# RoPE over 16 heads on one core: fp16 products summed by TensorE against fp32 throughout, in place, by VectorE, GpSimd and TensorE

## The chip, the cores and the metric

The kernel runs on one core of one Trainium2 chip. The metric is the device time of one execution in microseconds (us). The profile's span, from the first to the last instruction, is some 1.5 to 2 us shorter.

## The reference

```python
# x: (16, 512, 1024) float32, 16 heads of 64; cos, sin: (512, 32)
x = x.reshape(batch, seq, num_heads, head_dim)
x1, x2 = x[..., :half_dim], x[..., half_dim:]
cos, sin = cos[None, :, None, :], sin[None, :, None, :]
out = concatenate([x1 * cos - x2 * sin, x1 * sin + x2 * cos], axis=-1)
```

Every output is a sum of two products: a = x · cos, and b = (x with its halves exchanged) · (−sin, +sin). So 33.55 MB are read, 33.55 MB written, and each element costs two multiplications and an addition.

## The kernel before

The load, issued from GpSimd, converts fp32 to fp16 on its way. VectorE makes both products in fp16, a batch (128 partitions x 4096) at a time. TensorE adds them: two matmuls by the identity accumulate in PSUM, the memory that TensorE writes. (The tiles lie in SBUF, the core's other on-chip memory.) ScalarE copies the fp32 sum out.

```python
xin = ctx.enter_context(tc.tile_pool(name="xin", bufs=3))
tmp = ctx.enter_context(tc.tile_pool(name="tmp", bufs=2))
orez = ctx.enter_context(tc.tile_pool(name="orez", bufs=3))
# ... tables in fp16, identity in fp16 ...
for bo in range(batch // BP):                       # BP = 2 batches per load
    x_sb = xin.tile([P, BP, KK, dim], FP16)
    nc.gpsimd.dma_start(out=x_sb, in_=x_v2[bo])
    for bi in range(BP):
        # ...
        nc.vector.tensor_tensor(out=A, in0=xb, in1=cosb, op=ALU.mult)
        nc.vector.tensor_tensor(out=Bt, in0=swap_view(xb), in1=snsb, op=ALU.mult)
        for c in range(FREE // CH):                 # CH = 512
            nc.tensor.matmul(out=ps, lhsT=ident, rhs=Aflat[:, sl], start=True, stop=False)
            nc.tensor.matmul(out=ps, lhsT=ident, rhs=Bflat[:, sl], start=False, stop=True)
            nc.scalar.copy(out=oflat[:, sl], in_=ps)
        nc.sync.dma_start(out=out_v[b], in_=o_sb)
```

Of the kernel before, what the change touches and what calls it, by code (L numbers as in the profile page):

```python
# [1 line left out]

# [5 lines left out]

FP32 = mybir.dt.float32  # L10
FP16 = mybir.dt.float16
ALU = mybir.AluOpType


@with_exitstack
def kernel(
    ctx: ExitStack,
    tc: tile.TileContext,
    x: bass.AP,
    cos: bass.AP,  # L20
    sin: bass.AP,
    num_heads: bass.AP,
    out: bass.AP,
):
    nc = tc.nc
    P = nc.NUM_PARTITIONS
    batch, seq, dim = x.shape
    nh = num_heads
    head_dim = dim // nh
    half = head_dim // 2  # L30

    KK = seq // P
    assert P * KK == seq
    FREE = KK * dim
    CH = 512
    assert FREE % CH == 0
    BP = 2
    assert batch % BP == 0

    x_v2 = x.rearrange("(bo bi) (p kk) d -> bo p bi kk d", bi=BP, kk=KK)  # L40
    out_v = out.rearrange("b (p kk) h d -> b p kk (h d)", kk=KK)
    cos_v = cos.rearrange("(p kk) j -> p kk j", kk=KK)
    sin_v = sin.rearrange("(p kk) j -> p kk j", kk=KK)

    fixed = ctx.enter_context(tc.tile_pool(name="fixed", bufs=1))
    xin = ctx.enter_context(tc.tile_pool(name="xin", bufs=3))
    tmp = ctx.enter_context(tc.tile_pool(name="tmp", bufs=2))
    orez = ctx.enter_context(tc.tile_pool(name="orez", bufs=3))
    psum = ctx.enter_context(tc.tile_pool(name="psum", bufs=4, space=bass.MemoryType.PSUM))

    ident = fixed.tile([P, P], FP16)
    make_identity(nc, ident)

    cos_sb = fixed.tile([P, KK, half], FP32)
    sin_sb = fixed.tile([P, KK, half], FP32)
    nc.sync.dma_start(out=cos_sb, in_=cos_v)
    nc.sync.dma_start(out=sin_sb, in_=sin_v)
    cos16 = fixed.tile([P, KK, half], FP16)
    sns16 = fixed.tile([P, KK, 2, half], FP16)
    nc.vector.tensor_copy(out=cos16, in_=cos_sb)  # L60
    nc.vector.tensor_scalar_mul(out=sns16[:, :, 0, :], in0=sin_sb, scalar1=-1.0)  # L61
    nc.vector.tensor_copy(out=sns16[:, :, 1, :], in_=sin_sb)  # L62

    cosb = bass.AP(
        tensor=cos16.tensor,
        offset=cos16.offset,
        ap=[cos16.ap[0], [half, KK], [0, nh * 2], [1, half]],
    )
    snsb = bass.AP(
        tensor=sns16.tensor,  # L70
        offset=sns16.offset,
        ap=[sns16.ap[0], [2 * half, KK], [0, nh], [1, 2 * half]],
    )

    def swap_view(x_sb):
        return bass.AP(
            tensor=x_sb.tensor,
            offset=x_sb.offset + half,
            ap=[x_sb.ap[0], [head_dim, KK * nh], [-half, 2], [1, half]],
        )  # L80

    for bo in range(batch // BP):
        x_sb = xin.tile([P, BP, KK, dim], FP16)
        nc.gpsimd.dma_start(out=x_sb, in_=x_v2[bo])  # L84
        for bi in range(BP):
            b = bo * BP + bi
            xb = x_sb[:, bi]

            A = tmp.tile([P, KK, dim], FP16, name="A")
            nc.vector.tensor_tensor(out=A, in0=xb, in1=cosb, op=ALU.mult)  # L90
            Bt = tmp.tile([P, KK, dim], FP16, name="Bt")
            nc.vector.tensor_tensor(out=Bt, in0=swap_view(xb), in1=snsb, op=ALU.mult)  # L92

            o_sb = orez.tile([P, KK, dim], FP32)
            Aflat = A.rearrange("p kk d -> p (kk d)")
            Bflat = Bt.rearrange("p kk d -> p (kk d)")
            oflat = o_sb.rearrange("p kk d -> p (kk d)")
            for c in range(FREE // CH):
                sl = slice(c * CH, (c + 1) * CH)
                ps = psum.tile([P, CH], FP32)  # L100
                nc.tensor.matmul(out=ps, lhsT=ident, rhs=Aflat[:, sl], start=True, stop=False)  # L101
                nc.tensor.matmul(out=ps, lhsT=ident, rhs=Bflat[:, sl], start=False, stop=True)  # L102
                nc.scalar.copy(out=oflat[:, sl], in_=ps)  # L103

            nc.sync.dma_start(out=out_v[b], in_=o_sb)


# [1 line left out]
_INS = ['x', 'cos', 'sin', 'num_heads']  # L109
_OUTS = [((16, 512, 16, 64), 'float32')]  # L110
#: Inputs that are plain numbers.
_NUMBERS = {'num_heads': 16}


# [26 lines left out]
```

## Time and profile before

| | before |
|---|---|
| median time | 165.67 us (2 runs, 165.66 to 165.68) |
| span of the profiled run | 164.1 us |
| busiest engine | TensorE, 54% |
| transfers (both queues) | 98.5% of the 16 engines' span |

The page of the profile. The first lines give the span and each engine's busy time. The DMA row is the busy share of the transfer engines in 40 equal slices of the span, in tenths; the queue lines give packets, MB and share; the line that starts with "DMA 71%" is the chain of waits that ended last.

```profile
span 164.1 us, 814 instructions
PE 88.6 (54%) x256; PEld 31.5 (19%) x256; DVE 72.5 (44%) x35; ACT 68.7 (42%) x129; POOL 6.5 (4%) x14
...
DMA  5999999999999999999999999999999999999992
...
q0 software_dynamic: 2176, 16.78, 49.7%
q1 hardware_dynamic: 2592, 33.69, 48.8%
...
HBM read 33.69 MB, written 33.55 MB: 410 GB/s over the span
...
DMA 71%; PE 11%; ACT 6%; DVE 3%; issue 1%; ACTq 0%; POOL 0%; POOLq 0%; DVEq 0%
```

The DMA row is full from the second slice to the last but one, and the two queues together are at 98.5%. The 67.2 MB move at 410 GB/s (the load queue's 16.78 MB are counted after the conversion to fp16). No engine is over 54% busy. What bounds this kernel is the transfers, and nearly nothing else.

In the profile PE is TensorE, DVE VectorE, ACT ScalarE, POOL GpSimd, and L103 is a line of the kernel. Two groups of instructions matter for costing the change, from the same page (count, busy us and mean ns of one, then the idle time before it).

```profile
L103 ACT COPY o_sb<-ps 128x512 f32<-128x512 f32 x128 | 67.4, 609 | 82.9 <-DMA out_dram<-o_sb 58.5
L90 DVE TENSOR_TENSOR A<-x_sb,cos 128x4096 f16<-128x4096 f16 x16 | 36.7, 2291 | 69.9 <-DMA x_sb<-in_x_dram 41.3
```

ScalarE copies 512 columns in 609 ns, from which its copies of 1024 were estimated. VectorE takes 2.29 us for 4096 fp16 elements. The timeline of TensorE (start, duration, instruction, idle time before) shows how the clock falls during idle time:

```profile
72.49 0.58 PE L101 MATMUL ps<-A,ident 128*128 128x512 f16 x1 [4.21 <-ACT o_sb L103]
72.87 0.63 PE L102 MATMUL ps<-Bt,ident 128*128 128x512 f16 x1
73.30 0.63 PE L101 MATMUL ps<-A,ident 128*128 128x512 f16 x1
...
77.50 0.38 PE L101 MATMUL ps<-A,ident 128*128 128x512 f16 x1
77.72 0.38 PE L102 MATMUL ps<-Bt,ident 128*128 128x512 f16 x1
```

After 4.2 us of idleness a 512-column fp16 matmul starts every 0.43 us. Five microseconds later it starts every 0.22 us.

### The profile page before, as it was taken

How to read it: one execution, taken by the hardware profiler on the slowest of the kernel's cores; microseconds unless marked ns; L12 is line 12 of the kernel's file. 1: busy time of each engine (PE TensorE's matmuls, PEld its weight loads, DVE VectorE, ACT ScalarE, POOL GpSimd, SP SyncE). 2: the span in 40 equal slices, each digit the busy share in tenths (PEclk: the TensorE clock that was granted, in tenths of full speed). 3: DMA queues.
4: the chain of work that ended last, by engine and by line, in shares of the span. 5: the costliest groups of instructions: out<-in, count | busy, mean ns of one | idle time of the engine just before them, and what ended most of it. 6: DMA issues, size and time to landing. Idle time of an engine off the chain costs nothing.

```text
span 164.1 us, 814 instructions
## 1 busy us (share of the span) xinstructions
PE 88.6 (54%) x256; PEld 31.5 (19%) x256; DVE 72.5 (44%) x35; ACT 68.7 (42%) x129; POOL 6.5 (4%) x14
## 2 busy tenths in 40 slices
PE   0000599940954908639195491954919559986000
PEld 0000133310311302213032130311303123331000
DVE  1005979904880073900929037280733707950000
ACT  3000289811805409145080541806428075798100
POOL 7000010010001000010000100000000000000000
PEclk9999999998586585865858658586585855999955
DMA  5999999999999999999999999999999999999992
GB/s 90 196 218 222 220 208 180 290 332 326 312 312 330 324 298 336 306 308 346 310 312 312 326 328 306 326 308 326 326 316 316 304 403 423 413 435 443 423 423 92
DMA packets 4772, 50.51 MB, mean 308 GB/s; under 512 B 416, under 2 KB 672, under 8 KB 672
## 3 DMA queue, kind: packets, MB, share of 16 engines
q0 software_dynamic: 2176, 16.78, 49.7%
q1 hardware_dynamic: 2592, 33.69, 48.8%
q8 instruction: 2, 0.03, 0.1%
q14 instruction: 2, 0.02, 0.0%
HBM read 33.69 MB, written 33.55 MB: 410 GB/s over the span
## 4 chain that ended last, share of the span: by engine, by line
DMA 71%; PE 11%; ACT 6%; DVE 3%; issue 1%; ACTq 0%; POOL 0%; POOLq 0%; DVEq 0%
DMA out_dram<-o_sb 63%; DMA x_sb<-in_x_dram 8%; ACT o_sb L103 6%; PE ps L102 6%; PE ps L101 6%; DVE A L90 1%; DVE Bt L92 1%; ACTq L136 0%; POOL ident masks.py:197 0%; ACTq L103 0%; POOLq masks.py:199 0%; DVEq L90 0%; POOLq L122 0%
## 5 line engine op out<-in xcount | busy, mean ns | idle before, releaser
L103 ACT COPY o_sb<-ps 128x512 f32<-128x512 f32 x128 | 67.4, 609 | 82.9 <-DMA out_dram<-o_sb 58.5
L101 PE MATMUL ps<-A,ident 128*128 128x512 f16 x128 | 65.4, 519 | 60.8 <-ACT o_sb L103 43.6
L90 DVE TENSOR_TENSOR A<-x_sb,cos 128x4096 f16<-128x4096 f16 x16 | 36.7, 2291 | 69.9 <-DMA x_sb<-in_x_dram 41.3
L102 PE MATMUL ps<-Bt,ident 128*128 128x512 f16 x128 | 62.9, 506 | 1.6 <-DVE Bt L92 1.6
L92 DVE TENSOR_TENSOR Bt<-x_sb,sns 128x4096 f16<-128x4096 f16 x16 | 36.6, 2285 | 0.0
L102 PEld LDWEIGHTS <-ident 128*128 128x128 f16 x128 | 15.6, 122 | 87.0 <-issue 83.7
L101 PEld LDWEIGHTS <-ident 128*128 128x128 f16 x128 | 15.8, 124 | 32.1 <-issue 23.5
L84 POOL DMA_DIRECT2D x_sb<-in_x_dram x8 | 5.8, 730 | 83.9 <-DVE Bt L92 83.6
L103 ACT ACT_TABLE_LOAD x1 | 1.3, 1283 | 0.7 <-PEq L122 0.7
L60 DVE CAST cos<-cos_sb 128x128 f16<-128x128 f32 x1 | 0.2, 227 | 2.6 <-DMA cos_sb<-in_cos_dram 2.6
L61 DVE TENSOR_SCALAR sns<-sin_sb 128x128 f16<-128x128 f32 x1 | 0.5, 509 | 0.6 <-DMA sin_sb<-in_sin_dram 0.6
L62 DVE CAST sns<-sin_sb 128x128 f16<-128x128 f32 x1 | 0.4, 434 | 0.0
masks.py:199 POOL TENSOR_SCALAR_AFFINE_SELECT ident<-ident 128x128 f16<-128x128 f16 x1 | 0.3, 304 | 0.1
masks.py:197 POOL MEMSET ident<- 128x128 f16 x1 | 0.2, 205 | 0.3 <-POOLq L122 0.3
L122 POOL MEMSET const-float32-0.0<- 128x1 f32 x1 | 0.1, 93 | 0.2 <-issue 0.2
L122 POOL MEMSET const-bfloat16-1.0<- 128x1 bf16 x1 | 0.1, 95 | 0.0
L122 POOL MEMSET const-uint8-127<- 128x1 uint8 x1 | 0.1, 95 | 0.0
L122 POOL MEMSET const-float32-1.0<- 128x1 f32 x1 | 0.1, 93 | 0.0
## 6 DMA issues: line engine op xcount, KB each, us to landing
out_dram<-o_sb SPq DMA_DIRECT2D x16, 2048.0 KB, 23.5
x_sb<-in_x_dram POOLq DMA_DIRECT2D x8, 2048.0 KB, 40.3
cos_sb<-in_cos_dram SPq DMA_DIRECT2D x1, 64.0 KB, 1.8
sin_sb<-in_sin_dram SPq DMA_DIRECT2D x1, 64.0 KB, 2.2
```

The costliest lines, as they stand in the source:

```text
L60: nc.vector.tensor_copy(out=cos16, in_=cos_sb)
L61: nc.vector.tensor_scalar_mul(out=sns16[:, :, 0, :], in0=sin_sb, scalar1=-1.0)
L62: nc.vector.tensor_copy(out=sns16[:, :, 1, :], in_=sin_sb)
L84: nc.gpsimd.dma_start(out=x_sb, in_=x_v2[bo])
L90: nc.vector.tensor_tensor(out=A, in0=xb, in1=cosb, op=ALU.mult)
L92: nc.vector.tensor_tensor(out=Bt, in0=swap_view(xb), in1=snsb, op=ALU.mult)
L101: nc.tensor.matmul(out=ps, lhsT=ident, rhs=Aflat[:, sl], start=True, stop=False)
L102: nc.tensor.matmul(out=ps, lhsT=ident, rhs=Bflat[:, sl], start=False, stop=True)
L103: nc.scalar.copy(out=oflat[:, sl], in_=ps)
L122: nc = _bacc.Bacc("TRN2", target_bir_lowering=False, num_devices=1)
```

## The change

The intent is to work in fp32 from end to end, with fp32 loads from SyncE's hardware queue, large transfers (64 KB in a row per partition, four batches per tile), and the sum written over x, so that three tiles fit. A tile has 16 rows of 1024 per partition. In each row GpSimd makes b (VectorE in rows 6 and 14). In ten rows VectorE makes a in PSUM and adds b; in six rows VectorE multiplies x by cos in place, TensorE adds through the identity, and ScalarE copies back. The cos table, the a product and the sin table of rows 6 and 14 lie in PSUM, so that no VectorE instruction reads two operands from SBUF.

```diff
-    CH = 512
-    BP = 2
+NB = 4
+BUFS = 3
+PE_ROWS = (1, 4, 7, 9, 12, 15)
+DVE_B_ROWS = (6, 14)
# ... cut: views, tables ...
+    xp = ctx.enter_context(tc.tile_pool(name="xp", bufs=BUFS))       # 64 KB each
+    bp = ctx.enter_context(tc.tile_pool(name="bp", bufs=2))          # 4 KB each
+    pa = ctx.enter_context(tc.tile_pool(name="pa", bufs=2, space=bass.MemoryType.PSUM))
+    pe = ctx.enter_context(tc.tile_pool(name="pe", bufs=1, space=bass.MemoryType.PSUM))
+    ctx.enter_context(tc.manual_schedule())
# ... cut ...
+    def finish():
+        k, r, a, b = pending.pop(0)
+        if a is not None:
+            nc.vector.tensor_tensor(out=r, in0=a, in1=b, op=ALU.add)
+            return
+        nc.vector.tensor_tensor(out=pairs(r), in0=pairs(r), in1=cos_b(k), op=ALU.mult)
+        ps = pe.tile([P, dim], FP32, name="ps")
+        for c in range(0, dim, 512):
+            nc.tensor.matmul(out=ps[:, c : c + 512], lhsT=ident, rhs=r[:, c : c + 512], start=True, stop=False)
+            nc.tensor.matmul(out=ps[:, c : c + 512], lhsT=ident, rhs=b[:, c : c + 512], start=False, stop=True)
+        nc.scalar.copy(out=r, in_=ps)
+
+    for t in range(NT):
+        xt = tiles[t]
+        for k in range(KK):
+            r = xt[:, k * dim : (k + 1) * dim]
+            b = bp.tile([P, dim], FP32, name="b")
+            mul = nc.vector if k in DVE_B_ROWS else nc.gpsimd
+            mul.tensor_tensor(out=halves(b), in0=swapped(r), in1=sns_b(k, k in DVE_B_ROWS), op=ALU.mult)
+            a = None
+            if k not in PE_ROWS:
+                a = pa.tile([P, dim], FP32, name="pa")
+                nc.vector.tensor_tensor(out=pairs(a), in0=pairs(r), in1=cos_b(k), op=ALU.mult)
+            pending.append((k, r, a, b))
+            if len(pending) > 1:
+                finish()
+        while pending:
+            finish()
+        store(t)
+        if t == 1:
+            load(BUFS)
```

Loads 0 to 2 are issued at the start; load 3 (the fourth) is issued after the second store.

More of the change, by code (lines that the diff above doesn't have):

```diff
@@ L10 @@
 FP32 = mybir.dt.float32
-FP16 = mybir.dt.float16
 ALU = mybir.AluOpType
+NB = 4
+BUFS = 3
+PE_ROWS = (1, 4, 7, 9, 12, 15)
+DVE_B_ROWS = (6, 14)
 @with_exitstack
@@ L28 @@
     nh = num_heads
-    head_dim = dim // nh
-    half = head_dim // 2
-    KK = seq // P
-    assert P * KK == seq
-    FREE = KK * dim
-    CH = 512
-    assert FREE % CH == 0
-    BP = 2
-    assert batch % BP == 0
-    x_v2 = x.rearrange("(bo bi) (p kk) d -> bo p bi kk d", bi=BP, kk=KK)
-    out_v = out.rearrange("b (p kk) h d -> b p kk (h d)", kk=KK)
-    cos_v = cos.rearrange("(p kk) j -> p kk j", kk=KK)
-    sin_v = sin.rearrange("(p kk) j -> p kk j", kk=KK)
-    fixed = ctx.enter_context(tc.tile_pool(name="fixed", bufs=1))
@@ L46 @@
-    xin = ctx.enter_context(tc.tile_pool(name="xin", bufs=3))
-    tmp = ctx.enter_context(tc.tile_pool(name="tmp", bufs=2))
-    orez = ctx.enter_context(tc.tile_pool(name="orez", bufs=3))
-    psum = ctx.enter_context(tc.tile_pool(name="psum", bufs=4, space=bass.MemoryType.PSUM))
-    ident = fixed.tile([P, P], FP16)
-    make_identity(nc, ident)
-    cos_sb = fixed.tile([P, KK, half], FP32)
-    sin_sb = fixed.tile([P, KK, half], FP32)
-    nc.sync.dma_start(out=cos_sb, in_=cos_v)
-    nc.sync.dma_start(out=sin_sb, in_=sin_v)
@@ L58 @@
-    cos16 = fixed.tile([P, KK, half], FP16)
-    sns16 = fixed.tile([P, KK, 2, half], FP16)
-    nc.vector.tensor_copy(out=cos16, in_=cos_sb)
-    nc.vector.tensor_scalar_mul(out=sns16[:, :, 0, :], in0=sin_sb, scalar1=-1.0)
-    nc.vector.tensor_copy(out=sns16[:, :, 1, :], in_=sin_sb)
-    cosb = bass.AP(
-        tensor=cos16.tensor,
-        offset=cos16.offset,
-        ap=[cos16.ap[0], [half, KK], [0, nh * 2], [1, half]],
-    )
-    snsb = bass.AP(
-        tensor=sns16.tensor,
-        offset=sns16.offset,
-        ap=[sns16.ap[0], [2 * half, KK], [0, nh], [1, 2 * half]],
-    )
@@ L75, in swap_view @@
-    def swap_view(x_sb):
+    hd = dim // nh
+    half = hd // 2
+    PB = P // NB
+    KK = seq // PB
+    NT = batch // NB
+    F = KK * dim
+    x_v = x.rearrange("(t b) (p k) d -> t (b p) (k d)", b=NB, k=KK)
+    out_v = out.rearrange("(t b) (p k) h d -> t (b p) (k h d)", b=NB, k=KK)
+    cos_v = cos.rearrange("(p k) j -> p (k j)", k=KK)
+    sin_v = sin.rearrange("(p k) j -> p (k j)", k=KK)
+    fixed = ctx.enter_context(tc.tile_pool(name="fixed", bufs=1))
+    xp = ctx.enter_context(tc.tile_pool(name="xp", bufs=BUFS))
@@ new lines, with load @@
+    bp = ctx.enter_context(tc.tile_pool(name="bp", bufs=2))
+    pfix = ctx.enter_context(tc.tile_pool(name="pfix", bufs=1, space=bass.MemoryType.PSUM))
+    pa = ctx.enter_context(tc.tile_pool(name="pa", bufs=2, space=bass.MemoryType.PSUM))
+    pe = ctx.enter_context(tc.tile_pool(name="pe", bufs=1, space=bass.MemoryType.PSUM))
+    ctx.enter_context(tc.manual_schedule())
+    tiles = [None] * NT
+    stores = {}
+    def load(t):
+        tiles[t] = xp.tile([P, F], FP32, name="xt")
+        step = 2 * dim if t == 0 else F
+        for f in range(0, F, step):
+            nc.sync.dma_start(out=tiles[t][:, f : f + step], in_=x_v[t][:, f : f + step])
@@ new lines, in store @@
+    def store(t):
+        step = F // 4 if t == NT - 1 else F
+        for f in range(0, F, step):
+            nc.sync.dma_start(out=out_v[t][:, f : f + step], in_=tiles[t][:, f : f + step])
+    cos_sb = bp.tile([P, KK * half], FP32, name="b")
+    sin_sb = bp.tile([P, KK * half], FP32, name="b")
+    load(0)
+    for b in range(NB):
+        nc.scalar.dma_start(out=cos_sb[b * PB : (b + 1) * PB, :], in_=cos_v)
+        nc.scalar.dma_start(out=sin_sb[b * PB : (b + 1) * PB, :], in_=sin_v)
+    for t in range(1, BUFS):
+        load(t)
@@ new lines @@
+    ident = fixed.tile([P, P], FP32)
+    make_identity(nc, ident)
+    sns = fixed.tile([P, KK, 2, half], FP32)
+    sin_k = sin_sb.rearrange("p (k j) -> p k j", k=KK)
+    nc.vector.tensor_scalar_mul(out=sns[:, :, 0, :], in0=sin_k, scalar1=-1.0)
+    nc.vector.tensor_copy(out=sns[:, :, 1, :], in_=sin_k)
+    tab = pfix.tile([P, 512], FP32)
+    nc.vector.tensor_copy(out=tab[:, : KK * half], in_=cos_sb)
+    tab2 = pfix.tile([P, len(DVE_B_ROWS), hd], FP32)
+    for i, k in enumerate(DVE_B_ROWS):
+        nc.vector.tensor_copy(out=tab2[:, i], in_=sns[:, k].rearrange("p a j -> p (a j)"))
@@ L76, in swap_view, with cos_b, sns_b, swapped @@
+    def cos_b(k):
+        c = tab[:, k * half : (k + 1) * half]
+        return bass.AP(tensor=c.tensor, offset=c.offset, ap=[c.ap[0], [0, 2 * nh], [1, half]])
+    def sns_b(k, psum):
+        s = tab2[:, DVE_B_ROWS.index(k)] if psum else sns[:, k].rearrange("p a j -> p (a j)")
+        return bass.AP(tensor=s.tensor, offset=s.offset, ap=[s.ap[0], [0, nh], [1, hd]])
+    def swapped(r):
         return bass.AP(
-            tensor=x_sb.tensor,
-            offset=x_sb.offset + half,
-            ap=[x_sb.ap[0], [head_dim, KK * nh], [-half, 2], [1, half]],
-        )
@@ L82 @@
-    for bo in range(batch // BP):
-        x_sb = xin.tile([P, BP, KK, dim], FP16)
-        nc.gpsimd.dma_start(out=x_sb, in_=x_v2[bo])
-        for bi in range(BP):
-            b = bo * BP + bi
-            xb = x_sb[:, bi]
-            A = tmp.tile([P, KK, dim], FP16, name="A")
-            nc.vector.tensor_tensor(out=A, in0=xb, in1=cosb, op=ALU.mult)
-            Bt = tmp.tile([P, KK, dim], FP16, name="Bt")
-            nc.vector.tensor_tensor(out=Bt, in0=swap_view(xb), in1=snsb, op=ALU.mult)
-            o_sb = orez.tile([P, KK, dim], FP32)
-            Aflat = A.rearrange("p kk d -> p (kk d)")
-            Bflat = Bt.rearrange("p kk d -> p (kk d)")
-            oflat = o_sb.rearrange("p kk d -> p (kk d)")
-            for c in range(FREE // CH):
-                sl = slice(c * CH, (c + 1) * CH)
-                ps = psum.tile([P, CH], FP32)
-                nc.tensor.matmul(out=ps, lhsT=ident, rhs=Aflat[:, sl], start=True, stop=False)
-                nc.tensor.matmul(out=ps, lhsT=ident, rhs=Bflat[:, sl], start=False, stop=True)
-                nc.scalar.copy(out=oflat[:, sl], in_=ps)
-            nc.sync.dma_start(out=out_v[b], in_=o_sb)
+            tensor=r.tensor, offset=r.offset + half, ap=[r.ap[0], [hd, nh], [-half, 2], [1, half]]
+        )
@@ new lines, in pairs, with heads, halves @@
+    def pairs(r):
+        return r.rearrange("p (a j) -> p a j", j=half)
+    def heads(r):
+        return r.rearrange("p (h d) -> p h d", d=hd)
+    def halves(r):
+        return r.rearrange("p (h a j) -> p h a j", a=2, j=half)
+    pending = []
+    def finish():
[9 more added lines that the diff above has]
+        nc.scalar.copy(out=r, in_=ps)
```

## The prediction

> **What bounds it now.** The transfers. In the table of 40 slices the DMA row reads 9 in nearly every slice; the queue table gives the loads 49.7% and the stores 48.8% of the 16 engines' span; the chain of waits is 71% DMA. The header says 410 GB/s over 164.1 us for 67.2 MB. At 425 the same bytes need about 158 us, so the transfer side offers the change at most some 3%.
>
> **What the change does.** Bytes at HBM stay the same: an fp32 load still reads 33.5 MB. It removes fp16, and with it VectorE's fast mode: today 128x4096 fp16 takes 2.29 us, which is 0.16 us + 2 elements per cycle at 0.96 GHz. An fp32 row of 1024 at one element per cycle would take 0.157 + 1.067 = 1.22 us (estimate). VectorE gets 112 of these: 137 us instead of 73. GpSimd gets 56 two-input rows; no duration in this trace, so from the Trainium skill, "GPSIMD Engine Reference", section 3.1 (4497 ns for 2048 fp32): about 2.25 us each (estimate), 126 us. TensorE gets 96 fp32 matmuls of 512 columns; the skill's "FP8 and Floating Point Precision" gives true fp32 four passes. The timeline shows one fp16 pass every 0.213 us warm and 0.43 us after an idle gap of about 4 us, for the first 5 us; so 0.85 us warm, 1.7 us cold, 3.4 to 6.8 us per row (estimate). ScalarE: 24 copies of about 1.05 us (609 ns now for half the columns), harmless.
>
> Each engine's sum alone would fit under 160 us. The order does not let them overlap. Only two 4 KB buffers hold the product b, since three 64 KB tiles fill the partition. A TensorE row holds one of them from GpSimd's start until its fourth matmul ends. In the built order the rows in between all use the other buffer, so GpSimd writes (2.25), VectorE adds (1.22), GpSimd may write again; and the VectorE rows 6 and 14 wait for TensorE before they can write b, with VectorE standing. Walking the built order and its semaphores with the durations above gives about 55 us per four-batch tile with TensorE always warm and 61 us with gaps cold, against 39 us that one tile's load and store take. Compute becomes the critical path: 10 us until data and tables are there, 4 x 61, then the last quarter's store, 7 us. Transfers then idle in gaps.
>
> **Prediction: 260 us, 8 in 10 between 222 and 290.** Faster by over 2%: 0.02; within 2%: 0.02; slower: 0.96.
>
> **Where the profile would show it.**
> - DMA row of the slices: gaps; mean near 260 GB/s instead of 410.
> - Groups of instructions: VectorE fp32 row 1.2 us, GpSimd row 2.2 us, matmul 0.85 to 1.7 us, granted clock 0.5 to 0.8.
> - Waits: GpSimd on VectorE's add and on TensorE, VectorE on GpSimd, TensorE on VectorE, each tens of us. Chain of waits: GpSimd, VectorE and TensorE in turn, DMA under 20%.
> - Each tile's compute about 60 us; the last store quarter alone at the end.
>
> **What would make it wrong.** GpSimd rows near 1.1 us (then about 223). TensorE staying warm throughout (about 240), or fp32 running in one pass (about 210). GpSimd slower on the swapped, 32-element runs (3 us: about 290). To be faster than before, GpSimd, TensorE and VectorE would all have to beat these durations; even with GpSimd free the walk stays near 200.

## The result and the profile after

| | before | after |
|---|---|---|
| median time | 165.67 us | 275.79 us (2 runs, 275.53 to 276.05) |
| ratio | | 1.662 (95%: 1.649 to 1.674) |
| span | 164.1 us | 274.3 us |
| GB/s at HBM | 410 | 247 |

Ratios are the mean time of one kernel's runs over that of the other's of the same rounds, so they are not quite the ratio of the quoted medians. Executions over 1.5% slower than the fastest of the same kernel are left out of the means.

The same parts of the page, after:

```profile
span 274.3 us, 776 instructions
PE 133.5 (49%) x192; PEld 51.7 (19%) x192; DVE 133.6 (49%) x117; ACT 25.6 (9%) x25; POOL 131.4 (48%) x62
...
DMA  7999799990039930000039997930077991471007
...
q1 hardware_dynamic: 2592, 67.11, 57.9%
...
HBM read 34.08 MB, written 33.55 MB: 247 GB/s over the span
...
PE 37%; POOL 21%; DVE 17%; issue 15%; DMA 4%; ACT 2%; POOLq 1%
```

The transfers now have holes, some of them five slices long. They fell from 98.5% to 57.9% of the span for the same bytes, so they no longer bound anything. No engine is the limit by its sum either: TensorE, VectorE and GpSimd are each busy 48 or 49% of the span. Three engines that are each busy half of the time, and take turns on the chain (37%, 21% and 17%), are engines that wait for each other. The groups:

```profile
L133 POOL TENSOR_TENSOR b<-xt,sns 128x1024 f32<-128x1024 f32 x56 | 130.7, 2348 | 126.2 <-DVE xt L118 100.4
L123 PE MATMUL ps<-xt,ident 128*128 128x512 f32 x96 | 81.4, 946 | 132.4 <-DVE xt L120 97.3
L124 PE MATMUL ps<-b,ident 128*128 128x512 f32 x96 | 65.5, 773 | 0.0
L118 DVE TENSOR_TENSOR xt<-pa,b 128x1024 f32<-128x1024 f32 x40 | 48.2, 1222 | 34.7 <-POOL b L133 34.3
L133 DVE TENSOR_TENSOR b<-xt,tab 128x1024 f32<-128x1024 f32 x8 | 9.8, 1222 | 50.5 <-PE ps L124 50.5
```

L133 is the product b, L118 the add, L123 and L124 are TensorE's matmuls on x and on b (further down, L137 is the product a and L120 the multiplication in place). Each row costs about what was estimated: 1.22 us on VectorE, as said, and 2.35 us on GpSimd, where 2.25 was said. TensorE has 96 matmuls in the program and 192 in the trace, two for each. The waits, as "who waited for whom: us in total, times, longest":

```profile
POOL b L133 <- DVE xt L118: 100.4, 30, 9.2
PE ps L123 <- DVE xt L120: 97.3, 13, 17.7
DVE b L133 <- PE ps L124: 50.5, 8, 6.7
DVE xt L118 <- POOL b L133: 34.3, 19, 2.5
DVE xt L120 <- POOL b L133: 29.7, 23, 5.1
...
POOL b L133 <- PE ps L124: 15.4, 7, 5.4
```

The only wait of a compute engine for a transfer is that for the tables at the start (10.9 us). None waits for x. The timeline of the third tile shows one turn of the machine (start, duration, engine, line, instruction; in brackets the idle time before it and what ended it):

```profile
147.07 4.65 POOL L133 TENSOR_TENSOR b<-xt,sns 128x1024 f32<-128x1024 f32 x2 [1.34 <-DVE xt L118]
149.45 1.22 DVE L120 TENSOR_TENSOR xt<-xt,tab 128x1024 f32<-128x1024 f32 x1 [1.32 <-POOL b L133]
150.82 2.04 PE L123 MATMUL ps<-xt,ident 128*128 128x512 f32 x2 [6.39 <-DVE xt L120]
...
155.81 1.02 PE L124 MATMUL ps<-b,ident 128*128 128x512 f32 x2
156.87 1.22 DVE L133 TENSOR_TENSOR b<-xt,tab 128x1024 f32<-128x1024 f32 x1 [6.20 <-PE ps L124]
158.01 1.22 DVE L137 TENSOR_TENSOR pa<-xt,tab 128x1024 f32<-128x1024 f32 x1
159.14 2.35 DVE L118 TENSOR_TENSOR xt<-pa,b 128x1024 f32<-128x1024 f32 x2
160.44 4.65 POOL L133 TENSOR_TENSOR b<-xt,sns 128x1024 f32<-128x1024 f32 x2 [8.71 <-DVE xt L118]
```

At 147.07 GpSimd writes b for rows 4 and 5, one in each of the two buffers, and then has nowhere to write. Row 4 is a TensorE row. VectorE multiplies its x by cos (149.45), and TensorE works on it from 150.82 to 156.8; only then is row 4's buffer free. Meanwhile VectorE stands for 6.2 us. The next thing in its order is to write b of row 6 into that same buffer. Row 5 would only need an add, which would free the other buffer, but the add stands behind row 6's two products (156.87, 158.01) in VectorE's queue and runs at 159.14. So GpSimd stands for 8.7 us. The second and the third tile of 16 rows take 61.5 us each this way (stores issued at 79.2, 140.7 and 202.1 us). Whether another order of VectorE's instructions, with row 5's add ahead of row 6's products, would have freed the buffer sooner was not tested.

### The profile page after: what moved, and what is told of

Read it like the earlier page. It is cut to its first block, busy times and chain, and to the rows that moved or that the text cites. A ratio compares the mean times of both kernels' runs of the same rounds, so it can differ in the third digit from the quotient of the medians.

```text
span 274.3 us, 776 instructions
## 1 busy us (share of the span) xinstructions
PE 133.5 (49%) x192; PEld 51.7 (19%) x192; DVE 133.6 (49%) x117; ACT 25.6 (9%) x25; POOL 131.4 (48%) x62
## 3 DMA queue, kind: packets, MB, share of 16 engines
q1 hardware_dynamic: 2592, 67.11, 57.9%
## 4 chain that ended last, share of the span: by engine, by line
PE 37%; POOL 21%; DVE 17%; issue 15%; DMA 4%; ACT 2%; POOLq 1%
PE ps L123 22%; POOL b L133 21%; PE ps L124 16%; DVE xt L118 9%; DVE xt L120 5%; DVE pa L137 3%; ACT xt L125 2%; DMA b<-in_sin_dram 2%; DMA xt<-in_x_dram 2%; POOLq L176 1%; DVE b L133 0%; POOLq L133 0%
## 5 line engine op out<-in xcount | busy, mean ns | idle before, releaser
L133 POOL TENSOR_TENSOR b<-xt,sns 128x1024 f32<-128x1024 f32 x56 | 130.7, 2348 | 126.2 <-DVE xt L118 100.4
L123 PE MATMUL ps<-xt,ident 128*128 128x512 f32 x96 | 81.4, 946 | 132.4 <-DVE xt L120 97.3
L124 PE MATMUL ps<-b,ident 128*128 128x512 f32 x96 | 65.5, 773 | 0.0
L118 DVE TENSOR_TENSOR xt<-pa,b 128x1024 f32<-128x1024 f32 x40 | 48.2, 1222 | 34.7 <-POOL b L133 34.3
L123 PEld LDWEIGHTS ps<-xt,ident 128*128 128x128 f32 x96 | 25.2, 290 | 172.5 <-issue 143.2
L137 DVE TENSOR_TENSOR pa<-xt,tab 128x1024 f32<-128x1024 f32 x40 | 48.8, 1221 | 0.0
L125 ACT COPY xt<-ps 128x1024 f32<-128x1024 f32 x24 | 24.3, 1012 | 223.6 <-PE ps L124 223.6
L120 DVE TENSOR_TENSOR xt<-xt,tab 128x1024 f32<-128x1024 f32 x24 | 29.3, 1222 | 29.7 <-POOL b L133 29.7
L133 DVE TENSOR_TENSOR b<-xt,tab 128x1024 f32<-128x1024 f32 x8 | 9.8, 1222 | 50.5 <-PE ps L124 50.5
L124 PEld LDWEIGHTS ps<-b,ident 128*128 128x128 f32 x96 | 26.5, 276 | 40.8 <-issue 32.0
L83 DVE TENSOR_SCALAR sns<-b 128x512 f32<-128x512 f32 x1 | 0.4, 427 | 10.9 <-DMA b<-in_sin_dram 10.9
```

Source lines behind the costliest of these rows:

```text
L83: nc.vector.tensor_scalar_mul(out=sns[:, :, 0, :], in0=sin_k, scalar1=-1.0)
L118: nc.vector.tensor_tensor(out=r, in0=a, in1=b, op=ALU.add)
L120: nc.vector.tensor_tensor(out=pairs(r), in0=pairs(r), in1=cos_b(k), op=ALU.mult)
L123: nc.tensor.matmul(out=ps[:, c : c + 512], lhsT=ident, rhs=r[:, c : c + 512], start=True, stop=False)
L124: nc.tensor.matmul(out=ps[:, c : c + 512], lhsT=ident, rhs=b[:, c : c + 512], start=False, stop=True)
L125: nc.scalar.copy(out=r, in_=ps)
```

## The experiments

The theory: the two 4 KB buffers of b tie GpSimd, VectorE and TensorE into a chain, and TensorE's long, cold fp32 matmuls stretch that chain. The rivals: (1) the fp32 work is simply too much for the engines; (2) the four-pass matmuls alone are the loss; (3) the large tiles and the late fourth load starve the engines; (4) the build's choice of buffers is unlucky and a plain rotation would do. Where an expectation gives a number "by walking the built order", it is an estimate: each engine's instructions one after the other, in the order and with the semaphore waits of the built program, with the row times that the trace shows. All kernels gave correct results.

### 1. The control: room for more buffers

The partition is full: three tiles of 64 KB and 16 KB that the build reserves for the descriptors of transfers issued from GpSimd. The changed kernel issues none, so the reserve can shrink.

```diff
-    nc = _bacc.Bacc("TRN2", target_bir_lowering=False, num_devices=1)
+    nc = _bacc.Bacc("TRN2", target_bir_lowering=False, num_devices=1, dynamic_dma_scratch_size=1024)
```

> Control: the changed kernel with the reserved descriptor area at the bottom of each partition cut from 16 KB to 1 KB, and nothing else; still two b buffers. No DMA is issued from GpSimd, so nobody should use that area. Every theory expects the changed kernel's time, 276 us within 1%.

Measured: 276.06 us (one look, state unknown). Shrinking the reserve costs and gains nothing that this look shows. Every run below with three or five b buffers carries this edit too.

### 2. Three and five b buffers

```diff
-    bp = ctx.enter_context(tc.tile_pool(name="bp", bufs=2))
+    bp = ctx.enter_context(tc.tile_pool(name="bp", bufs=5))    # and in another run: bufs=3
```

> The control with three b buffers in place of two. Theory (two buffers chain GpSimd, VectorE and TensorE): walking the built order with the measured row times gives a span of about 201 us if TensorE stays as cold as it was, about 190 if it stays warm; GpSimd's wait for VectorE's add falls from 100 us to under 40. Rival 1 (the fp32 work itself is too long for the engines) and rival 2 (slow four-pass matmuls alone): within 5% of 276, because no engine's work changes.

> The control with five b buffers. Theory: about 182 us (span 180): the chain is gone, each four-batch tile takes about 35 us of compute, VectorE and GpSimd are over 70% busy, and what is left over 166 is the first data, VectorE's own sum and the last quarter's store. Rivals 1 and 2: 276 within 5%.

Measured: 200.63 us with three (ratio 1.210, 1.204 to 1.216) and 176.64 us with five (1.066, 1.063 to 1.070). No instruction was added or taken away; 12 KB of buffer (three of 4 KB) gave back 99 of the 110 us. With three, GpSimd's wait for VectorE's add fell from 100 us to 11; the span, 199.4 us, met the expected 201 partly by luck, since TensorE was warmer than that walk assumed (granted clock 0.849) while GpSimd also waited 10 us for the fourth load. This refutes rival 1 and shows the theory's main claim. The page and the waits with five buffers:

```profile
PE 99.4 (57%) x192; PEld 38.6 (22%) x192; DVE 130.3 (74%) x117; ACT 25.6 (15%) x25; POOL 130.5 (74%) x62
```

```profile
POOL b L133 <- DMA xt<-in_x_dram: 18.0, 2, 17.1
DVE pa L137 <- DMA xt<-in_x_dram: 14.8, 1, 14.8
```

VectorE and GpSimd are now at 74%, and the long waits for each other are gone. The 18.0 and 14.8 us that are left are waits for the fourth load, which were hidden before (see 6). Five buffers came out 5 us better than expected; the next run suggests why.

### 3. No row through TensorE, with two and with five buffers

```diff
-PE_ROWS = (1, 4, 7, 9, 12, 15)
+PE_ROWS = ()
```

> The changed kernel, two b buffers, but no row goes through TensorE: VectorE adds all sixteen rows of a tile. VectorE's sum rises from 137 to 166 us. Theory: a buffer is then held for 1.2 us by an add instead of 5 to 8 us by TensorE, the chain shortens although VectorE has more to do: about 194 us. Rival 1 (too much fp32 work, VectorE first of all): slower than 276, by up to the 29 us added to VectorE. Rival 2 (slow matmuls alone): also faster, so this run does not tell it from the theory; the runs with more buffers do.

> No row through TensorE, and five b buffers. Theory: with no TensorE row, a buffer is only held for one add, so two buffers were nearly enough: 182 to 187 us, at most 1% from the run without TensorE rows and with two buffers, because VectorE (136 row operations) is now the limit. If buffers were worth the same by themselves (100 us, or a third of the time), this run would fall far below it.

Measured: 184.36 us with two buffers (1.113, 1.111 to 1.115) and 183.60 us with five (1.108, 1.107 to 1.110). Together with 2 this makes a square:

| median us | six TensorE rows per tile | no TensorE row |
|---|---|---|
| two b buffers | 275.79 | 184.36 |
| five b buffers | 176.64 | 183.60 |

Three more buffers are worth 99 us where TensorE holds them, and 0.8 us where it does not. Taking TensorE's help away made the two-buffer kernel 91 us faster, though VectorE has 24 more rows to do. With five buffers the same help is worth 7 us. So it is neither the buffers alone nor the TensorE rows alone, but the two together; sections 4 and 5 test that it is the time for which a TensorE row holds one of two buffers. One more thing differs between the two-buffer kernels: without TensorE rows the build gives out the buffers nearly in turn. That choice does not explain the 91 us, since with TensorE rows strict turns are slower still (section 5).

The first run was expected at 194 and came in at 184. The timeline of VectorE tells a part of why (start, duration):

```profile
59.00 1.23 DVE L137 TENSOR_TENSOR pa<-xt,tab 128x1024 f32<-128x1024 f32 x1
60.14 1.22 DVE L118 TENSOR_TENSOR xt<-pa,b 128x1024 f32<-128x1024 f32 x1
61.39 1.23 DVE L137 TENSOR_TENSOR pa<-xt,tab 128x1024 f32<-128x1024 f32 x1
62.53 1.22 DVE L118 TENSOR_TENSOR xt<-pa,b 128x1024 f32<-128x1024 f32 x1
```

Each row is listed with 1.22 us, but two rows follow each other at 1.13 to 1.25 us, 1.18 on average (ten rows from 59.00 to 70.83). The recorded durations overlap where the next instruction had nothing to wait for. Summing durations overstated VectorE by a few per cent; 136 rows at 1.22 us are 166 us, and the profile has it busy for 161.3. That is some 5 of the 10 us; the rest is not accounted for.

### 4. Shorter matmuls: fp16 products in the TensorE rows

```diff
+        r16 = r.bitcast(FP16)[:, :dim]          # the products of these rows, written in place
+        b16 = b.bitcast(FP16)[:, :dim]
-            nc.tensor.matmul(out=ps[:, c : c + 512], lhsT=ident, rhs=r[:, c : c + 512], start=True, stop=False)
-            nc.tensor.matmul(out=ps[:, c : c + 512], lhsT=ident, rhs=b[:, c : c + 512], start=False, stop=True)
+            nc.tensor.matmul(out=ps[:, c : c + 512], lhsT=ident16, rhs=r16[:, c : c + 512], start=True, stop=False)
+            nc.tensor.matmul(out=ps[:, c : c + 512], lhsT=ident16, rhs=b16[:, c : c + 512], start=False, stop=True)
```

> The changed kernel with two b buffers, but in the six TensorE rows of a tile the two products are written as fp16 (in place), so that each matmul is one pass, not four; VectorE and GpSimd do the same number of rows. Precision falls in these rows to that of the kernel before; the result must still pass. Theory: TensorE holds a b buffer about 1.7 us in place of 6, but GpSimd and VectorE still take turns in the other buffer: about 207 us. Rival 2 (the slow four-pass matmuls are the whole loss): below 180. Rival 1 (too much work for VectorE and GpSimd): near 276.

Measured: 208.13 us (1.257, 1.255 to 1.258). But this run had a second difference. Buffers are given out when the program is built, by what the build believes to be free, and with shorter matmuls it gave the rows other buffers. The run was repeated with the changed kernel's choice fixed row by row (building both programs again gives the same string of buffers):

```diff
+    slots = iter("ABBABBBABABBAAAB...")   # as the changed kernel was built
+    bps = {c: ctx.enter_context(tc.tile_pool(name="bp" + c, bufs=1)) for c in "AB"}
-            b = bp.tile([P, dim], FP32, name="b")
+            b = bps[next(slots)].tile([P, dim], FP32, name="b")
```

> The run with fp16 products had a second difference that its edit does not show: the build chose other buffers for the rows (the two b buffers nearly in turn, where the changed kernel uses one of them for three rows running). Here the fp16 products keep the changed kernel's choice, row by row. Theory: 222 to 226 us, so of the 68 us that the fp16 run gained some 15 came from the choice of buffers. If the choice does not matter: 208.

Measured: 222.39 us (one look, state unknown). So the passes themselves are worth 53 us of the 110, and 14 of the 68 us of the first run came from the other buffers. Rival 2 is refuted: with matmuls of a quarter of the work the kernel is still 57 us slower than before.

These shorter matmuls ran cold from first to last, one every 0.40 to 0.43 us (start, duration, from the second run):

```profile
102.53 0.63 PE L128 MATMUL ps<-b,ident 128*128 128x512 f16 x1
102.96 0.63 PE L127 MATMUL ps<-xt,ident 128*128 128x512 f16 x1
```

The record gives a mean granted clock of 1.0 for both fp16 runs, but their traces hold no clock record at all. Whether TensorE was warm is read from the starts of its matmuls, not from that mean.

### 5. The buffers in turn, and TensorE kept warm

Rival 4, with the two buffers fixed in strict turns ("ABAB..."):

> The changed kernel with its two b buffers used strictly in turn, row after row. Rival 4 (the build's odd choice of buffers is what holds the engines up, and a plain rotation would not): clearly faster than 276, towards 200. Theory (two buffers are too few in any order while TensorE holds one for 6 us or more): slower still, about 300 us, since GpSimd then waits for TensorE at every second row after a TensorE row.

Measured: 300.49 us (one look, state unknown), so the build's choice was better than the plain rotation; GpSimd's wait for TensorE's matmuls rose from 15 to 73 us.

Then TensorE's clock. With the buffers fixed as built, sixteen matmuls of zeros were put where TensorE stood idle:

```diff
         nc.scalar.copy(out=r, in_=ps)
+        if k in (1, 4, 9, 12):
+            idle = pe.tile([P, dim], FP32, name="ps")
+            for _ in range(16):
+                nc.tensor.matmul(out=idle[:, :512], lhsT=warm[:, :P], rhs=warm, start=True, stop=True)
```

> The changed kernel with its two b buffers, each row's buffer fixed to the one the changed kernel's build gave it, and sixteen idle fp16 matmuls of zeros after rows 1, 4, 9 and 12 of each tile, into the free PSUM tile, which nobody reads; they fill most of the 6 to 7 us in which TensorE stood there. Nothing else has more or less to do. Theory: the granted clock rises from 0.73 to over 0.9, a row's four matmuls take 3.7 us in place of 6.0, and as TensorE is on the chain the time falls to 243 us (span 242). If TensorE were off the critical path: 276.

Measured: 249.21 us (1.505, 1.499 to 1.511), at a granted clock of 0.931 instead of 0.728. More work on TensorE made the kernel 27 us faster, so TensorE is on the chain, and its cold clock was worth about a quarter of the loss. The expectation had every row warm. Ten of the 24 TensorE rows still began cold and took some 5.1 to 5.9 us, which is enough to cover the 6 us that are missing. The timeline of TensorE shows both kinds:

```profile
132.90 3.61 PE L133 MATMUL ps<-warm 128*128 128x512 f16 x16 [1.10 <-ACT xt L129]
138.20 1.10 PE L127 MATMUL ps<-xt,ident 128*128 128x512 f32 x2 [1.69 <-DVE xt L124]
...
142.97 3.61 PE L133 MATMUL ps<-warm 128*128 128x512 f16 x16 [1.10 <-ACT xt L129]
149.22 2.05 PE L127 MATMUL ps<-xt,ident 128*128 128x512 f32 x2 [2.64 <-DVE xt L124]
151.06 1.54 PE L128 MATMUL ps<-b,ident 128*128 128x512 f32 x2
152.44 1.02 PE L127 MATMUL ps<-xt,ident 128*128 128x512 f32 x2
```

After a gap of 1.69 us (138.20) the row stayed warm, 3.7 us for its four matmuls; after one of 2.64 us (149.22) it began cold and took 5.1. This is not a threshold: with five buffers a row turned cold after a gap of 2.00 us (at 58.35), and in the last version below one stayed warm after 3.73 us (at 122.62).

### 6. The order of the transfers, with two and with five buffers

```diff
         store(t)
-        if t == 1:
+        if t == 0:
             load(BUFS)
```

> The changed kernel with two b buffers and one change of order on the transfer queue: the fourth load is issued after the first store and ahead of the second. Rival 3 (three large tiles and the late fourth load starve the engines of data): clearly faster, by up to the 20 us that a store takes. Theory: 273 to 276, as no engine waited for x.

> Five b buffers and the fourth load ahead of the second store. In the run with five b buffers GpSimd stood 17 us and VectorE 15 us until the fourth load had landed. Theory: that wait goes, the transfers stay busy from the first load to the last store, and the time is what 67 MB need: 165 to 168 us, so the change without its hold-ups comes back to the kernel before, not below it by 2%.

Measured: 272.87 us with two buffers (one look, state unknown). Even these 3 us do not speak for rival 3. They all lie in the fourth tile (compute of 61.4 us in place of 65; the third store was issued at 202.3, before at 202.1), no engine waited for x in either run, and building both programs again shows that the edit also gave the fourth tile other b buffers: those of the tiles that took 61.5. With five buffers, 169.60 us (1.024, 1.022 to 1.026), 7 us better than without the edit, but above the expected 165 to 168. The waits for the fourth load are gone (0.8 us left on GpSimd). What was left, by stretches of time (window, length, busy time of the engines, granted clock, DMA share, GB/s):

```profile
84.00:86.00 2.00, 0.97 (x3) 0.49 (x4) 2.00 (x3) 0.98 (x1) 2.00 (x2) 1.00 1.37 459
86.00:88.00 2.00, 2.00 (x6) 0.94 (x5) 1.95 (x2) 0.00 (x0) 2.00 (x2) 1.00 0.16 66
```

From 86 to 88 us the transfers were at 0.16. The fourth load needs the buffer that the first store frees, and nothing was queued behind that store. The last version stores the first half of the second tile ahead of the fourth load:

```diff
+            if t == 1 and k == 8:
+                store(1, 0, F // 2)
+                load(BUFS)
         while pending:
             finish()
-        store(t)
-        if t == 0:
-            load(BUFS)
+        store(t, F // 2 if t == 1 else 0)      # tile 1 in quarters; load 0 in 4 pieces
```

> The run with five b buffers and the early fourth load left the transfers nearly empty around 82 to 88 us, as the queue had nothing behind the first store until it had ended. Here the first half of the second tile is stored ahead of the fourth load, so that the queue always holds two transfers; the first load comes in four pieces in place of eight. Theory: 2 to 4 us less than the 169.6 of that run, 166 to 167.5 us, which is the kernel before within 1%.

Measured: 167.36 us (1.010, 1.008 to 1.012), the same as before at the 2% threshold. The hole is filled (the first load's pieces were changed too, so the 2.2 us gained are not shown to be the hole's alone):

```profile
84.00:86.00 2.00, 0.90 (x3) 0.44 (x3) 2.00 (x3) 1.01 (x1) 2.00 (x2) 1.00 0.88 377
86.00:88.00 2.00, 2.00 (x6) 0.81 (x5) 1.95 (x3) 0.00 (x0) 2.00 (x2) 1.00 0.99 426
```

The transfers are at 95.5% on the main queue and 1.2% on that of the tables. So the fp32 design can be brought back to the kernel before, and stays some 1.7 us above it. Where these last 1.7 us go was not tested; no version beat the kernel before.

## Why the prediction was right

The measured 275.79 us lie in the stated range of 222 to 290, and the direction was clear. Step by step:

- **The transfers bound the kernel before.** Right: 98.5% of the span. The last fp32 version needs 167.4 us and has its transfers over 96% busy. What faster transfers could give was not tested; no version here was faster than the kernel before.
- **VectorE rows at 1.22 us.** Right in duration (1222 ns on average). As a term of a sum it is 1.18, because recorded durations overlap.
- **GpSimd rows at 2.25 us**, half of what the Trainium skill ("GPSIMD Engine Reference", section 3.1) gives for twice the elements. Measured 2348 ns, 4% more.
- **fp32 as four passes**, from the skill's "FP8 and Floating Point Precision", section "TensorE Precision Notes". The trace agrees: each fp32 matmul is recorded as two instructions that start 0.43 us apart when warm, 0.86 us for 512 columns against 0.22 for one fp16 pass (warm starts in the kernel before lie 0.215 to 0.217 us apart; the prediction's 0.213 is not in that trace).
- **Two buffers tie the engines together.** Shown by 2 and 3, and by the waits: GpSimd for VectorE's add 100 us, VectorE for TensorE before it can write b 50 us.
- **Compute takes the chain, transfers idle.** Right: 247 GB/s (260 was said), DMA 4% of the chain (under 20% was said).
- **The centre was 260, 16 us too low.** The prediction's sum, 10 + 4 x 61 + 7, is 261 for a span that was 274.3. The mis-sized term is the compute of the first and the last tile. The second and the third took 61.5 us each, so the walk with gaps cold, 61, was right for them: in the third tile four of six TensorE rows began cold and took 6.0 to 6.2 us, and the two that came right after a ScalarE copy took 3.7. But the first store was issued at 79.2 us, after 67 us of compute from the first GpSimd row at 11.8, and the last tile ended with its compute at about 267, after 65. The head was 11.8 in place of 10, the end 7.4 in place of 7. For the last tile the cause is on record: its first two rows had two different b buffers, where the two tiles before had one and the same for both, and with their choice it took 61.4 (section 6). The first tile has the last one's choice with the two buffers exchanged; that this is what cost its 6 us was not tested.
- **What would have made it wrong.** "TensorE staying warm: about 240" was nearly tried: 249 with most, not all, rows warm. "One pass: about 210" was tried with fp16 products: 208, but 222 with the same buffers, so that part of the agreement was luck. GpSimd rows of 1.1 us or of 3 us could not be tried.

## What to carry to other kernels

When three engines pass rows along, first compare how long each step holds a buffer with how many buffers there are; the sums of busy time say nothing about it, as here, where three engines were each busy for half of the span of a kernel that was 66% slower. An engine whose next instruction must write into a buffer held elsewhere also holds back the instruction behind it that would free another one, as VectorE did here for 6.2 us. Before giving an engine work "because it is idle", ask what that work will hold and for how long at the clock that this engine really gets; and after mending the chain look at the transfers' order again, since the slow chain had hidden it.

## What the Trainium skill lacked or had wrong

- "TensorE: Matmul & The Clock Gate", section "What's actually happening": it gives about 3.4 us both for an idle window that makes TensorE cold and for the sustained work that makes it warm. Here the length of the listed gap did not decide: with five buffers a row turned cold after 2.00 us, and in the last version one stayed warm after 3.73. In the kernel before a burst ran cold for 5.0 us. The page does say that the window runs free of the kernel; no run here isolates that.
- "GPSIMD Engine Reference", section 3.1: 2.6 cycles per element would be 2.22 us for 1024 fp32 at 1.2 GHz (estimate); the rows with exchanged halves of 32 took 2.34 to 2.37 us. Whether the difference is a fixed cost of each instruction, for which that section's table has no number, or the exchange, no run here shows.
- "SBUF — State Buffer", section "Who interferes with whom", says that a VectorE instruction with at most one SBUF input outside its two-port modes does not contend with GpSimd. The trace agrees: GpSimd's 56 rows all lie within 2340 to 2368 ns beside VectorE rows of 1215 to 1226 ns. No run here has a VectorE row with two SBUF inputs to set against it.
- "SBUF — State Buffer", section "SBUF size: 192, 224, or 256?", counts 16 KiB of every partition as reserved for descriptors, and no page says that the reserve can be cut where GpSimd issues no transfer; with 1 KB in place of 16 KB the kernel ran correctly and in the same time (276.06 us).
